# Silu in the mixer written as x·(1 + tanh(x/2)), with the product on VectorE

## The chip, the cores and the metric

The kernel runs on one core of a Trainium2 chip. Five engines work beside each other, each through its own queue in order: TensorE (PE, with its weight loads PEld), VectorE (DVE), ScalarE (ACT), GpSimd (POOL) and SyncE (SP, which only issues DMAs). An instruction that waits holds up everything behind it on its engine. The metric is the device time of one execution in microseconds; lower is better.

## The reference

One decoder layer on 512 tokens of width 1024, in float32: a SwiGLU feed-forward block, a mixer of three branches (sparse attention, gated DeltaNet, cross-attention into a memory), and a second feed-forward block. What matters here are three places of the mixer with a silu, silu(x) = x·sigmoid(x):

```python
qkv = silu(causal_depthwise_conv(dn_qkv, dn_conv_w))          # 4 taps, 3 x 4 heads x 128 channels
dq, dk, dv = split(qkv);  dq = l2_norm(dq);  dk = l2_norm(dk) # x * rsqrt(sum(x*x) + 1e-6), per head
beta = sigmoid(dn_b)
o_dn = gated_delta_rule(dq, dk, dv, log_decay, beta)          # v enters as v*beta, k as k*beta*exp(g)
o_dn = rms_norm(o_dn, dn_out_norm) * silu(dn_z)               # the output gate
# compression of keys and values in the sparse attention:
silu(blocks @ w1) @ w2
```

The feed-forward blocks have a silu too; it is not touched.

## The kernel before

**Products.** Weights are streamed from HBM in tiles of 128 x 512: SP loads the tile (`wraw`, L105), ACT rounds it to a short float (`whi`, L106), DVE, or POOL for some tiles, forms the rest (`wlo`, L109). Each product in full precision is then a triple of matmuls, high by high (L117), high by low (L118, L119). One projection of 512 columns is 8 tiles of the contraction, 24 matmuls of 512 columns into one PSUM bank (`pfm`), or, where tokens are in the partitions, into four banks (`ptm`).

**DeltaNet.** For each of 4 heads there are three convolutions (s = 0, 1, 2 for q, k, v). `dn_conv` projects into a PSUM bank, DVE multiplies it by the last tap (`cacc`, through L229) and adds the other three (L844), all reading that bank, and ACT applies Silu into `cy`. `dn_head` transposes `cy` on PE into `ptr` (L862). For v, DVE multiplies by beta into `vb`. For q and k, ACT squares with a sum (`sq`, L874), DVE takes 1/sqrt by nine tiny steps (L138 to L148) and scales (`qs` or `kn`, L880), PE transposes back (`ptk`, L887), ACT copies (L888). `dn_rows` loads a head's cumulative log decays to all partitions by a DMA from DRAM (`rowsb`, L896, on SP's queue); ACT takes `eg` = exp of it (L899), POOL subtracts and masks (L900, L901), ACT takes `dec` = exp (L902). `dn_lt` multiplies k by beta on POOL (`kbT`), PE forms k·kᵀ (`pkk`, L931), DVE multiplies by `dec` and a DMA stores it; `dn_subst` loads it for two heads (`Lb`), inverts 16 x 16 blocks by substitution on DVE (30 small instructions, `Bt` and `Bi`, L951, L953, each waiting for the one before), stores the result (`dD`, L955, issued in ACT's queue) and loads it spread out (`Dc`); `dn_double` and `dn_level` start from `Dm`, made of `Dc` on DVE (L971). `in_z` projects the output gate into four banks and ACT applies Silu (`zg`, L787). `compress` does the same on 128 x 256 (`hs`, L1159) and transposes on.

**Buffers.** `cy` has 3 buffers, `cacc` 2, `rowsb`, `eg`, `dec` and `kn` 1 each. The projections' banks come in turn from a few tags of PSUM.

**Order.** The steps are given as a list of names in the table at L37: `i` the first products, `a` the scalars (beta, decays), `c01` the convolution of head 0, s = 1, `h01` its `dn_head`, `r0` the rows, `l0` and `k0` what follows, `b0` the substitution of heads 0 and 1, `z` the output gate, `e`, `d`, `s` the doubling, levels and states, `x`, `p`, `f` the compression. Each has an offset of priority and a number that says every how many weight tiles POOL makes `wlo`. From these, and from its own estimate of each instruction's duration, the framework's scheduler deals the instructions into the engines' queues at build time. So another duration or another instruction shifts the order of all that stands around it. The table itself is the same before and after.

## Time and profile before

| | |
|---|---|
| median of 3 runs | 1307.05 us (1304.54 to 1307.46) |
| the profiled execution | 1297.11 us, span 1295.3 us |
| DeltaNet's convolutions, heads, substitution | about 400 to 545 us of the span |
| levels, states, compression | about 545 to 690 us |

The profile is of one execution, which was itself shorter than the runs' median. A row of a group reads: line of the kernel, engine, operation, output <- inputs, shape, count | busy time in us, mean ns | idle time of the engine just before these instructions, and what ended it. A row of a timeline reads: start, duration, engine, line, operation; in brackets the idle time before it and what was waited for. [...]

[...]

### The profile page before, as it was taken

What the parts mean: (1) busy time and instruction counts of PE and PEld (TensorE: products, weight loads), DVE (VectorE), ACT (ScalarE), POOL (GpSimd) and SP (SyncE); (2) the same over time, 40 slices, a digit from 0 to 9 for tenths busy, and PEclk for the clock granted to TensorE, in tenths of its full rate; (3) what the DMA queues carried; (4) which work ended last, traced back from release to release, by engine and by line L of the source; (5) the groups of instructions that cost most, each with busy time, mean ns of one, the idle gap of its engine ahead of it and who ended that gap; (6) DMA issues with size and microseconds to landing.
All of it is one profiled execution on the core that took longest, in us unless ns stands there. A gap on an engine that the chain in (4) does not pass through costs nothing. (4 is left out here: it accounts for less than half of the span.)

```text
span 1295.3 us, 21771 instructions
## 1 busy us (share of the span) xinstructions
PE 1267.4 (98%) x7959; PEld 1102.6 (85%) x7959; DVE 978.2 (76%) x1778; ACT 734.8 (57%) x1487; POOL 213.1 (16%) x225
## 2 busy tenths in 40 slices
PE   8999999999999999999999999999999999999997
PEld 7889999988787778888777788899788899999886
DVE  6898878699877865845789776665688788785988
ACT  6566666576765644416564545544576566655663
POOL 0021112130002222002111112232200121110300
PEclk8999999999999999999999999999999999999999
DMA  7757656695663341333221142232843786664963
GB/s 238 250 173 186 179 179 125 195 220 202 228 198 106 111 125 50 85 114 117 65 58 58 58 138 66 82 115 94 276 167 117 257 189 187 183 128 152 235 223 113
DMA packets 112123, 195.61 MB, mean 151 GB/s; under 512 B 18973, under 2 KB 28561, under 8 KB 112017
## 3 DMA queue, kind: packets, MB, share of 16 engines
q1 hardware_dynamic: 95856, 159.36, 37.3%
q0 software_dynamic: 15872, 34.61, 13.8%
q8 instruction: 62, 1.02, 0.3%
q10 hardware_dynamic: 288, 0.26, 0.1%
q14 instruction: 45, 0.36, 0.1%
HBM read 184.15 MB, written 33.08 MB: 168 GB/s over the span
## 5 line engine op out<-in xcount | busy, mean ns | idle before, releaser
L106 ACT CAST whi<-wraw 128x512 fp32r<-128x512 f32 (+1 forms) x226 | 136.4, 615 | 133.6 <-PE pfm L119 61.3
L109 DVE TENSOR_TENSOR wlo<-wraw,whi 128x512 fp32r<-128x512 f32 (+1 forms) x195 | 133.8, 697 | 48.1 <-ACT whi L106 46.9
L536 POOL DMA_DIRECT2D T<-in_ffn_d_dram x88 | 59.5, 677 | 375.2 <-PE pg L119 111.7
L117 PE MATMUL pfm<-xth,whi 128*128 128x512 f32 x272 | 108.1, 402 | 2.0 <-ACT whi L106 0.9
L118 PE MATMUL pfm<-xth,wlo 128*128 128x512 f32 x272 | 108.5, 404 | 1.3 <-POOL wlo L109 1.3
L119 PE MATMUL pfm<-xtl,whi 128*128 128x512 f32 x272 | 107.9, 402 | 0.0
L109 POOL TENSOR_TENSOR wlo<-wraw,whi 128x512 fp32r<-128x512 f32 x28 | 38.2, 1366 | 229.5 <-ACT whi L106 165.4
L446 PE MATMUL smm<-thi,fset 128*128 128x256 f32 x384 | 67.9, 276 | 0.0
L117 PEld LDWEIGHTS pfm<-xth,whi 128*128 128x128 f32 x272 | 51.1, 189 | 13.0 <-issue 1.8
L466 DVE TENSOR_TENSOR up<-s,smm 128x256 f32<-128x256 f32 x32 | 13.5, 422 | 61.7 <-ACT se L461 61.7
L118 PEld LDWEIGHTS pfm<-xth,wlo 128*128 128x128 f32 x272 | 50.9, 188 | 10.6 <-POOL wlo L109 1.8
L119 PEld LDWEIGHTS pfm<-xtl,whi 128*128 128x128 f32 x272 | 50.9, 188 | 9.6 <-issue 0.8
L446 PEld LDWEIGHTS smm<-thi,fset 128*128 128x128 f32 x384 | 58.0, 188 | 0.2
L655 ACT CAST ringh<-ringr 128x1024 fp32r<-128x1024 f32 (+1 forms) x44 | 45.1, 1032 | 22.0 <-PE acc_mm L673 6.7
L446 PE MATMUL smm<-thi,fxtl 128*128 128x256 f32 x192 | 53.2, 277 | 0.7 <-DVE fxtl L421 0.7
L446 PE MATMUL smm<-thi,fxth 128*128 128x256 f32 x192 | 53.0, 276 | 0.0
L446 PE MATMUL se<-thi,fset 128*128 128x256 f32 x256 | 45.2, 276 | 0.0
L1256 ACT ACTIVATE Pm<-Pm,nm 128x384 f32<-128x384 f32 (+2 forms) x64 | 35.6, 558 | 14.6 <-DVE nm L1255 14.1
L688 DVE TENSOR_TENSOR sl<-H,sh 128x1024 fp32r<-128x1024 f32 (+2 forms) x38 | 40.9, 1082 | 3.1 <-ACT sh L687 2.9
L673 PE MATMUL acc_mm<-ringh,sh 128*128 128x512 f32 x108 | 42.3, 391 | 0.0
L673 PE MATMUL acc_mm<-ringh,sl 128*128 128x512 f32 x108 | 42.1, 390 | 0.0
L687 ACT CAST sh<-H 128x1024 fp32r<-128x1024 f32 (+2 forms) x38 | 35.3, 935 | 11.6 <-PE acc_r L673 3.6
(626 smaller groups left out, 4336.4 us busy)
## 6 DMA issues: line engine op xcount, KB each, us to landing
T<-in_ffn_d_dram POOLq DMA_DIRECT2D x88, 256.0 KB, 4.2
fq<-in_ffn_g_dram SPq DMA_DIRECT2D x64, 256.0 KB, 3.4
fq<-in_ffn_u_dram SPq DMA_DIRECT2D x64, 256.0 KB, 3.8
wraw<-in_ffn_g_dram SPq DMA_DIRECT2D x34, 256.0 KB, 3.2
wraw<-in_ffn_u_dram SPq DMA_DIRECT2D x34, 256.0 KB, 3.5
wraw<-in_ffn_d_dram SPq DMA_DIRECT2D x34, 256.0 KB, 3.7
ringr<-T SPq DMA_DIRECT2D x16, 512.0 KB, 6.6
ringr<-in_ffn_d_dram POOLq DMA_DIRECT2D x16, 512.0 KB, 8.9
```

Of the source, the lines that this page charges most:

```text
L106: nc.scalar.copy(hi, raw)
L109: self.lmark = eng.tensor_tensor(lo, raw, hi.bitcast(F32), op=OP.subtract)
L117: t.matmul(out, lh, rh, start=first, stop=False)
L118: t.matmul(out, ll, rh, start=False, stop=False)
L119: self.tick(t.matmul(out, lh, rl, start=False, stop=last), 3 * math.prod(out.shape[1:]))
L446: m = lambda x, y, **kw: te.matmul(out, x, y, skip_group_check=True, **kw)
L536: i = g.dma_start(o[c], x[c], max_dma_last_dim=2048, **({"accum_op": OP.add} if add else {}))
L655: nc.scalar.copy(hi, raw)
L673: e = lambda a, b, s, f: nc.tensor.matmul(acc[i], a, b, start=s, stop=f, skip_group_check=True)
L687: nc.scalar.copy(hi, f)
L688: last = tt(low, f, hi.bitcast(F32), op=OP.subtract)
L1256: nc.scalar.activation(pm, pm, AF.Exp, bias=nm[:, qb : qb + 1], scale=-1.0, accum_out=sm[:, qb : qb + 1])
```

## The change

Since silu(x) = x·(1 + tanh(x/2))/2, each of the three places becomes a Tanh on ACT with scale 0.5 and one DVE instruction (t + 1)·x (lines 789, 850 and 1164 of the changed kernel), which yields twice the silu. The factor 2 is taken out later: `hb`, half of beta, for v; 4·EPS for EPS in the norm of q and k, which is otherwise indifferent to a factor; the gain of the output norm halved once after its load (`dnog`); 0.5 in the copy of `hT`. The factor of k in the delta rule, `nbg`, keeps beta.

```diff
     def in_z(self, uh, ul, zg):
...
-            nc.scalar.activation(zg[:, b].rearrange("p h d -> p (h d)"), p, AF.Silu)
+            z = zg[:, b].rearrange("p h d -> p (h d)")
+            nc.scalar.activation(z, p, AF.Tanh, scale=0.5)
+            nc.vector.scalar_tensor_tensor(z, z, 1.0, p, op0=OP.add, op1=OP.mult)
     def dn_scalars(self, sm, mp):
...
-        nbg = t("nbg")
+        nbg, hb = t("nbg"), t("hb")
+        v.tensor_scalar(hb, beta, 0.5, None, op0=OP.mult)
...
-        return sg, gb[:, :16].rearrange("p (n h) -> p n h", h=4), beta, nbg, dr
+        return sg, gb[:, :16].rearrange("p (n h) -> p n h", h=4), hb, nbg, dr
     def dn_conv(self, h, s, uh, ul):
...
-        nc.scalar.activation(y, ac, AF.Silu)
+        nc.scalar.activation(y, ac, AF.Tanh, scale=0.5)
+        v.scalar_tensor_tensor(y, y, 1.0, ac, op0=OP.add, op1=OP.mult)
     def dn_head(self, h, s, y, sc, dp, d):
...
-                v.tensor_tensor(d["vb"], p, beta[:, :, h, None].to_broadcast(T4), op=OP.mult)
+                v.tensor_tensor(d["vb"], p, hb[:, :, h, None].to_broadcast(T4), op=OP.mult)
...
-        r = self.rsqrt(ss, TB, 1.0, EPS, "dr")
+        r = self.rsqrt(ss, TB, 1.0, 4 * EPS, "dr")
     def compress(self, ph, cm, op_):
...
-        nc.scalar.activation(hs, ph, AF.Silu)
+        nc.scalar.activation(hs, ph, AF.Tanh, scale=0.5)
+        nc.vector.scalar_tensor_tensor(hs, hs, 1.0, ph, op0=OP.add, op1=OP.mult)
...
-        nc.vector.tensor_copy(hT, pt.rearrange("p (k w c) -> p k w c", k=2, w=2))
+        nc.vector.tensor_scalar(hT, pt.rearrange("p (k w c) -> p k w c", k=2, w=2), 0.5, None, op0=OP.mult)
                def small():
                     nc.sync.dma_start(self.cw, a["conv_w"])
                     nc.sync.dma_start(self.dnog, a["dn_og"])
+                    nc.vector.tensor_scalar(self.dnog, self.dnog, 0.5, None, op0=OP.mult)
```

The lines below the first edit move by 2 to 6. The compiled program has 17 table loads before and 3 after.

The instructions move, in the DeltaNet part above all. Three places are shown. The first is ACT's queue from the first convolution's activation to the third's (cy is the activation of a convolution, sq the squares of a norm, eg and dec the decays, whi a rounded weight tile, k the copy of the transposed k). Before:

```order
374 L846 ACT_TABLE_LOAD
375 L846 ACTIVATE cy<-cacc 128x512
376 L106 CAST whi<-wraw 128x512
377 L874 ACTIVATE sq,dss<-ptr_4474 128x128 x4
378 L106 CAST whi<-wraw 128x512
379 L899 ACT_TABLE_LOAD
380 L899 ACTIVATE eg<-rowsb 128x512
381 L902 ACTIVATE dec<-dec 128x512
382 L846 ACT_TABLE_LOAD
383 L846 ACTIVATE cy<-cacc 128x512
384 L888 COPY k<-ptk 128x512
385 L106 CAST whi<-wraw 128x512 x2
```

And with the change:

```order
374 L849 ACTIVATE cy<-cacc 128x512
375 L106 CAST whi<-wraw 128x512
376 L878 ACTIVATE sq,dss<-ptr_4478 128x128 x4
377 L106 CAST whi<-wraw 128x512
378 L903 ACTIVATE eg<-rowsb 128x512
379 L849 ACTIVATE cy<-cacc 128x512
380 L906 ACTIVATE dec<-dec 128x512
381 L106 CAST whi<-wraw 128x512
382 L892 COPY k<-ptk 128x512
383 L106 CAST whi<-wraw 128x512
```

The second convolution's activation stands between eg and dec instead of behind dec, and a weight tile follows dec at once.

The second is DVE's queue at the same place, the end of the first k norm (small steps drm, dry, drz; kn is the scaled k). Before:

```order
463 L145 SCALAR_TENSOR_TENSOR dry<-drz,dry 128x4
464 L146 TENSOR_TENSOR drz<-dry 128x4
465 L147 SCALAR_TENSOR_TENSOR drz<-drz,drm 128x4
466 L148 SCALAR_TENSOR_TENSOR dry<-drz,dry 128x4
467 L880 TENSOR_TENSOR kn<-ptr_4474,dry 128x512
468 L229 TENSOR_SCALAR cacc<-pfm,cw 128x512
```

And with the change:

```order
466 L145 SCALAR_TENSOR_TENSOR dry<-drz,dry 128x4
467 L850 SCALAR_TENSOR_TENSOR cy<-cy,cacc 128x512
468 L146 TENSOR_TENSOR drz<-dry 128x4
469 L147 SCALAR_TENSOR_TENSOR drz<-drz,drm 128x4
470 L148 SCALAR_TENSOR_TENSOR dry<-drz,dry 128x4
471 L229 TENSOR_SCALAR cacc<-pfm,cw 128x512
472 L884 TENSOR_TENSOR kn<-ptr_4478,dry 128x512
```

The second convolution's product now stands inside the norm, and the scale of the third convolution ahead of kn. On PE the four transposes of kn come five matmuls later than before.

The third is DVE's queue at the end of the first substitution, with the change; before, the pairs of Bt and Bi ran to the end with one wlo between them, and Dm (there L971) followed with no convolution open.

```order
592 L957 TENSOR_TENSOR Bi<-Bi,Bt 64x3x13
593 L789 SCALAR_TENSOR_TENSOR zg<-zg,ptm 128x512
594 L955 TENSOR_TENSOR Bt<-Lb,Bi 64x28
595 L789 SCALAR_TENSOR_TENSOR zg<-zg,ptm 128x512
596 L957 TENSOR_TENSOR Bi<-Bi,Bt 64x2x14
597 L789 SCALAR_TENSOR_TENSOR zg<-zg,ptm 128x512
...
604 L847 SCALAR_TENSOR_TENSOR cacc<-pfm,cw,cacc 128x509
605 L975 TENSOR_TENSOR Dm<-Dc,msk 128x512 x2
606 L975 TENSOR_TENSOR DT<-Dc,msk 128x512
607 L847 SCALAR_TENSOR_TENSOR cacc<-pfm,cw,cacc 128x510
608 L789 SCALAR_TENSOR_TENSOR zg<-zg,ptm 128x512
609 L847 SCALAR_TENSOR_TENSOR cacc<-pfm,cw,cacc 128x511
```

Three products of the output gate lie in the substitution, and Dm stands between the taps of the ninth convolution. ACT issues the DMA dD behind three tanh of the gate, where before it stood ahead of the gate's activations. The DMA of the third head's rowsb comes two weight tiles later on SP's queue. From about 620 us of the span on, the order is as before.

## The prediction

> **What bounds the kernel now.** I read the summary of engines first, then the busy time by stages, then TensorE's waits in the stage that is touched.

> ```profile
> span 1295.3 us, 21771 instructions
> PE 1267.4 (98%) x7959; PEld 1102.6 (85%) x7959; DVE 978.2 (76%) x1778; ACT 734.8 (57%) x1487; POOL 213.1 (16%) x225
> ```

> PE works in 98% of the span, so an edit on ACT and DVE can only gain where PE stands still for one of them. The changed instructions run almost all between 400 and 620 us. In the windows below the columns are stretch, length, then busy PE, PEld, DVE, ACT, POOL with counts, PE's clock, DMA share and GB/s.

> ```profile
> 400.00:475.60 75.60, 69.91 (x343) 56.57 (x343) 57.52 (x143) 42.49 (x92) 20.84 (x20) 1.00 0.37 110
> 475.60:545.00 69.40, 68.64 (x426) 58.07 (x425) 49.30 (x142) 28.64 (x72) 10.39 (x13) 1.00 0.24 70
> 545.00:620.00 75.00, 74.49 (x481) 61.02 (x480) 41.65 (x109) 30.80 (x79) 14.82 (x16) 1.00 0.38 117
> ```

> PE's idle time is 75.60 - 69.91 = 5.69, then 0.76, then 0.51: 6.96 us in all. That is the ceiling of any gain, whatever the edit takes off ACT. ACT is idle for 44% of the first window and more than half of the others. PE's waits in 400 to 620 us, grouped (total, times, longest):

> ```profile
> PE ptk L887 <- DVE Bi L953: 1.7, 1, 1.7
> PE pfm L118 <- POOL wlo L109: 1.3, 1, 1.3
> PE ptk L887 <- DVE qs L880: 1.0, 2, 0.9
> PE pfm L117 <- ACT whi L106: 0.9, 1, 0.9
> PE pkk L931 <- POOL kbT L909: 0.7, 1, 0.7
> ```

> Of these 5.6 us only the 0.9 names ACT. 2.7 name DVE, which gets more to do, and 2.0 name POOL.

> **ACT's side.** The operations removed and replaced:

> ```profile
> L846 ACT ACT_TABLE_LOAD x6 | 7.7, 1283 | 0.1
> L899 ACT ACT_TABLE_LOAD x4 | 5.1, 1283 | 1.4 <-DMA rowsb<-drows 1.3
> L902 ACT ACT_TABLE_LOAD x2 | 2.6, 1283 | 0.0
> L846 ACT ACTIVATE cy<-cacc 128x512 f32<-128x512 f32 x12 | 7.6, 632 | 3.1 <-DVE cacc L844 2.9
> L1332 ACT ACTIVATE tg<-up 128x512 f32<-128x512 f32 x7 | 4.4, 625 | 0.0
> L787 ACT ACTIVATE zg<-ptm 128x512 f32<-128x512 f32 x4 | 2.1, 604 | 0.0
> ```

> Silu and Exp alternate in this stage, and each change of function puts a load of 1.283 us ahead. The order below has 14 fewer loads: these 12, one before zg and one at L1200. 14 x 1.283 = 18.0 us of ACT go. The Tanh that stands in for Silu costs the same: the kernel has it already (tg, 625 ns against 632 for cy).

> [...]

> **DVE's side.** Each Tanh gets a product (t + 1)·x on DVE. The same operation is in the trace at L1337, from SBUF and PSUM; L844 is the next.

> ```profile
> L1337 DVE SCALAR_TENSOR_TENSOR tg<-tg,pfm 128x512 f32<-128x512 f32 x16 | 10.3, 682 | 6.3 <-ACT tg L1332 3.6 <-POOL wlo L109 2.7
> L844 DVE SCALAR_TENSOR_TENSOR cacc<-pfm,cw,cacc 128x511 f32<-128x511 f32 x12 | 9.0, 746 | 0.2
> L951 DVE TENSOR_TENSOR Bt<-Lb,Bi 64x15 f32<-64x15 f32 x4 | 0.7, 166 | 0.4 <-DMA Lb<-dL 0.3
> ```

> The z products are L1337's form: 4 x 0.68 = 2.7. The convolutions' product reads two SBUF operands; I take 0.69, with 0.75 as upper bound: 12 x 0.69 = 8.3, at most 9.0. The compression's, half as wide, is at most 0.4 and the two small ones (beta and the norm's gain halved) are about 0.2 each, by the 166 ns of a tiny operation. Together 11.8 us. The other edits ride in instructions that exist: 4·EPS for EPS is a constant, and halved beta is another operand, so they cost nothing. The copy of hT is one DVE pass as before.

> [...]

> ```profile
> 462.98 1.05 DVE L951 TENSOR_TENSOR Bt<-Lb,Bi 64x55 f32<-64x55 f32 x1
> 462.50 1.47 POOL L916 TENSOR_TENSOR kd<-kn,dec 128x512 f32<-128x512 f32 x1 [3.44 <-DVE Bi L953]
> 468.64 0.21 DVE L951 TENSOR_TENSOR Bt<-Lb,Bi 64x55 f32<-64x55 f32 x1
> ```

> The same instruction takes 1.05 while POOL works, 0.21 otherwise: 0.84 for a collision. POOL is busy 46.05 of these 220 us (20.84 + 10.39 + 14.82), 21%, so of 12 products some 2.5 meet it: 2 us more on DVE, not on PE's path unless DVE is late there. [...]

> **Where PE feels it.** The instruction order around these stages is dealt anew, so I walked the queues.

> *First head's k, 407 to 420 us.* In this listing come start, duration, engine, instruction.

> ```profile
> 408.17 1.28 ACT L899 ACT_TABLE_LOAD   x1
> 410.82 0.63 ACT L899 ACTIVATE eg<-rowsb 128x512 f32<-128x512 f32 x1 [1.37 <-DMA rowsb<-drows]
> 413.39 0.63 ACT L902 ACTIVATE dec<-dec 128x512 f32<-128x512 f32 x1 [1.94 <-POOL dec L901]
> 414.04 1.28 ACT L846 ACT_TABLE_LOAD   x1
> 415.34 0.63 ACT L846 ACTIVATE cy<-cacc 128x512 f32<-128x512 f32 x1
> 416.34 1.14 ACT L106 CAST whi<-wraw 128x512 fp32r<-128x512 f32 x2
> 409.57 0.17 DVE L146 TENSOR_TENSOR drz<-dry 128x4 f32<-128x4 f32 x1
> 410.17 0.69 DVE L880 TENSOR_TENSOR kn<-ptr,dry 128x512 f32<-128x512 f32 x1
> 410.50 0.39 PE L119 MATMUL pfm<-xtl,whi 128*128 128x512 f32 x1
> 410.92 0.66 PE L887 MATMUL ptk<-cst,kn 128*128 128x128 f32 x4
> 415.54 0.39 PE L117 MATMUL pfm<-xth,whi 128*128 128x512 f32 x1
> 415.76 0.39 PE L118 MATMUL pfm<-xth,wlo 128*128 128x512 f32 x1
> 417.01 0.50 PE L117 MATMUL pfm<-xth,whi 128*128 128x512 f32 x1 [0.86 <-ACT whi L106]
> 419.08 0.50 PE L118 MATMUL pfm<-xth,wlo 128*128 128x512 f32 x1 [1.33 <-POOL wlo L109]
> ```

> Here the load does hurt: after dec ends at 414.02, load and cy and a copy keep the next whi until 416.34, and PE waits 0.86 and, behind it for the rest of that weight, 1.33. In the new order whi follows dec at once, at 414.0, 2.3 us earlier, and both waits go: 2.2 us, with the restarts about 2.5.

> But the new order hangs something else there. DVE's queue holds the product of the second convolution between the fourth and the fifth small step of the k norm (behind L145). Its tanh stands on ACT behind eg, and eg still waits for the DMA rowsb until 410.82. So: tanh 411.4 to 412.0, product to 412.7, the norm's three last steps 0.6 (410.17 - 409.57), a scale of the next convolution 0.7 that is now also ahead, kn at 414.0, and the transposes 0.75 later (410.92 - 410.17): 414.75. PE has five matmul rows more in front, which start 0.22 apart (415.54, 415.76), so it comes at 410.73 + 5 x 0.22 = 411.8. A new wait of 2.9 us. Term: 2.9 - 2.5 = +0.4. If tanh and product slip in earlier than I think, it falls to -2.5; if POOL collides with the product, it is +1.2.

> *The q and k norms behind.* The transposes of qs (1.0 in two waits) come once one product later, 0.68 at most, of which I take 0.4 (PE has as many rows in front as before); at the other place the order has 18 rows of the next convolution ahead of them, and that wait of 0.9 goes. kbT (0.7): +0.2, one product in the k chain less the loads. The 1.7 behind Bi: DVE has the product there too and PE five rows fewer, but the small steps of the norm are no longer interleaved with the substitution: -0.3. Sum: -0.6, bounds -2.5 and +1.5.

> *The output gate, from 460 us.*

> ```profile
> 471.76 0.67 ACTq L955 DMA_DIRECT2D dD<-Bi  x1
> 475.00 2.07 ACT L787 ACTIVATE zg<-ptm 128x512 f32<-128x512 f32 x4
> 477.98 2.16 DVE L971 TENSOR_TENSOR Dm<-Dc,msk 128x512 f32<-128x512 f32 x2 [3.49 <-DMA Dc<-dD]
> 406.50 2.73 SPq L105 DMA_DIRECT2D wraw<-in_w_dn_dram  x2
> ```

> Two things make the substitution later. The third head's row DMA stands two weight loads further back on SP, 2.73 us by the last row, and the substitution waits for the decays made from it; with the squares behind eg I take 4 us. Then three of the four zg products lie inside the substitution's last steps, 3 x 0.68 = 2.0. The DMA dD, which ACT now issues behind three tanh, goes from 471.76 to 477.8, and Dm from 477.98 to about 484. PE itself does not use Dm at once. But the ninth convolution's DVE work now lies around Dm: the bank that it reads comes free at 484 + 2.8 (Dm, DT) + 2 x 0.75 + 0.68 = 489. PE wants that bank two convolutions later: 475.7 + 2 x 24 x 0.22 = 486.3, with transposes between about 488. Term: +1.0. The ninth convolution itself needs a z bank that is freed by the first zg product, and that sits behind most of the substitution: +0.5, bounds 0 and +2.3.

> *The rest.* L1200's load lies where PE waits for DVE, not for it: 0. The compression's tanh and product: ACT's 0.38 becomes 0.8, beside PE's projections: 0. Without that cover it would cost 0.4.

> **Sum.** +0.4 - 0.6 + 1.0 + 0.5 = +1.3 us. The profiled execution took 1297.11, with 1.8 around its span of 1295.3; it would take 1298.4. The median of the runs is 1307.05, 9.9 above that execution, and I carry that over: 1308.4.

> **The rivals.** *Faster:* the loads were what made everything late, and the new waits do not arise, since tanh and product follow closer than I walked. Then the 0.9 and 1.3, with restarts 2.5, most of the 1.0 and half of the 1.7 go: about -4, 1303; -7 at the very most. For it: the chain at 414 to 419 shows a load on PE's path. Against it: 1.7 + 1.0 of the waits name DVE.

> *Slower, by the substitution:* dD is issued not at 477.8 but later, since DVE (busy 57.52 of 75.60 in that window, plus some 8 us of products, so 87%) meets POOL and stands behind the tanh of z, in its own queue. From about 479 on, each microsecond comes through to PE, by the ninth convolution's bank and then by the products that read Dm. With 3 to 4 us more of delay: +1.3 + 3.5 = about +5, 1312. For it: DVE would be the densest engine after PE there, and stalls in order. Against it: behind 475.6 PE idles 0.76 of 69.40 in the old order, so this stage has had slack. [...]

> *Nothing:* ACT was idle enough and DVE too, the schedules cancel, 1307; it falls within the forecast's bounds.

> **How the numbers follow.** What a measurement of this kernel can tell from no change is about 0.2%, 2.6 us. The forecast and the case of nothing, both within that: 0.42. Faster: 0.23. Slower, by the substitution or by the first head's wait at its upper bound: 0.35, more than the faster case, since three of four terms that I could walk point there. The likeliest case alone spans 1305.5 to 1311 by its bounds; with the rivals, 1302.5 to 1313.5.

> **What would show it.** Three table loads are left, ACT's busy time falls by about 18, DVE's rises by about 12. PE has a wait of 2 to 3 us at ptk <- kn near 412 to 415, and none for whi and POOL's wlo near 417. dD is issued near 478, and PE waits about 1 us for cacc in the third convolution after z. It would be wrong if ptk <- kn waits under 1 us (then the faster case), if PE's idle time in 475 to 545 grows beyond 3 us (the slower one), or if the products run far from 0.69.

## The result, and the profile after

The changed kernel is slower: its median is 1318.18 us (8 runs, 1310.66 to 1321.64) against 1305.16 for the kernel before (8 runs, 1298.33 to 1307.46). The ratio is 1.0111, 95% interval 1.0086 to 1.0137. The forecast of 1308.4 with a range up to 1313.5 was too low. The profiled execution took 1317.94.

The summary of engines of the changed kernel, and the three windows that the prediction showed of before (stretch, length, busy PE, PEld, DVE, ACT, POOL with counts, PE's granted clock, DMA share, GB/s):

```profile
span 1316.2 us, 21780 instructions
PE 1281.4 (97%) x7959; PEld 1112.0 (84%) x7959; DVE 993.1 (75%) x1797; ACT 717.2 (54%) x1473; POOL 213.6 (16%) x225
...
400.00:475.60 75.60, 66.29 (x319) 53.67 (x318) 59.10 (x133) 29.38 (x79) 19.47 (x18) 0.97 0.34 99
475.60:545.00 69.40, 66.49 (x384) 55.83 (x382) 52.41 (x131) 20.54 (x47) 11.74 (x15) 0.98 0.27 77
545.00:620.00 75.00, 73.15 (x482) 58.15 (x482) 41.39 (x134) 23.51 (x79) 8.13 (x9) 1.00 0.27 84
```

ACT's busy time falls by 17.6 us and DVE's rises by 14.9. ACT has 1473 instructions where it had 1487: the 14 loads are gone. The groups of the changed instructions:

```profile
L849 ACT ACTIVATE cy<-cacc 128x512 f32<-128x512 f32 x12 | 7.5, 628 | 12.2 <-DVE cacc L847 12.2
L850 DVE SCALAR_TENSOR_TENSOR cy<-cy,cacc 128x512 f32<-128x512 f32 x12 | 9.0, 754 | 3.7 <-ACT cy L849 3.6
```

The Tanh costs what the Silu did (628 against 632 ns). So the work changed as planned, and the time did not follow.

To find the loss I cut out one stage: from PE's first product with the running sums of the decays (`pgc`) to its first product of the compressed attention (`pcl`). Before, and after:

```profile
400.01 0.40 PE L820 MATMUL pgc<-ld,cst 128*128 128x16 f32 x2 [0.33 <-DVE ld L817]
606.63 1.00 PE L1194 MATMUL pcl<-cbd,qT 128*128 128x64 f32 x8
...
400.01:606.63 206.62, 200.18 (x1182) 165.28 (x1183) 137.03 (x369) 92.56 (x222) 41.72 (x45) 1.00 0.31 94
```

```profile
403.62 0.40 PE L822 MATMUL pgc<-ld,cst 128*128 128x16 f32 x2 [0.33 <-DVE ld L819]
623.34 1.00 PE L1199 MATMUL pcl<-cbd,qT 128*128 128x64 f32 x8
...
403.62:623.34 219.72, 205.98 (x1181) 168.01 (x1182) 151.88 (x386) 76.03 (x209) 42.51 (x45) 0.98 0.30 88
```

The stage takes 13.1 us longer (219.72 - 206.62), close to the difference of the medians (13.0). The two profiled executions as wholes lie further apart, 20.9 us (1316.2 - 1295.3): runs of the same kernel differ by several us, and the profiled one of before was shorter than its median. So below I compare this stage. PE's idle time in it goes from 6.44 to 13.74, +7.3; the rest, +5.8, is PE at work for longer on the same matmuls. PE's waits after:

```profile
PE ptk L891 <- DVE Bt L955: 3.5, 1, 3.5
PE ptk L891 <- DVE kn L884: 3.3, 1, 3.3
PE ptk L891 <- DVE qs L884: 1.5, 1, 1.5
PE pkk L935 <- POOL kbT L913: 1.3, 2, 0.7
PE pfm L117 <- DVE cacc L847: 1.2, 1, 1.2
PE pot L1064 <- DVE on L1058: 1.0, 1, 1.0
```

The first row is the third k norm, the second the first. At the first, the timeline reads:

```profile
414.17 0.63 ACT L903 ACTIVATE eg<-rowsb 128x512 f32<-128x512 f32 x1 [2.41 <-DMA rowsb<-drows]
414.70 0.61 ACT L849 ACTIVATE cy<-cacc 128x512 f32<-128x512 f32 x1
415.35 0.69 DVE L850 SCALAR_TENSOR_TENSOR cy<-cy,cacc 128x512 f32<-128x512 f32 x1 [2.40 <-ACT cy L849]
415.96 1.22 DVE L146 TENSOR_TENSOR drz<-dry 128x4 f32<-128x4 f32 x1
418.89 0.66 PE L891 MATMUL ptk<-cst,kn 128*128 128x128 f32 x4 [3.26 <-DVE kn L884]
...
416.29:419.70 3.41, 0.81 (x6) 0.78 (x7) 3.31 (x7) 1.26 (x3) 2.29 (x4) 1.00 0.00 0
419.70:423.11 3.41, 3.41 (x10) 2.64 (x9) 2.20 (x3) 1.61 (x3) 3.41 (x3) 0.50 0.26 79
```

The DMA's wait is handed on: eg waits 2.41 for it, the tanh stands behind eg, the product behind the tanh, the rest of the norm behind the product, and PE waits 3.26. The small step L146 (415.96 to 417.18) also took 1.22 instead of 0.17 while POOL worked (L905, 415.41 to 417.17). And then comes what I had not priced: the granted clock falls to 0.50 for the 3.41 us of the last row, in which PE is busy throughout. In it the matmuls of 512 columns start 0.43 us apart (419.95, 420.38), at clock 1.00 they start 0.23 apart with records of 0.39 that overlap (413.42, 413.65). By the granted clock such a dip loses half its length, 1.7 us, which is an estimate; by the starts it would be 1.6. The stage has two after, here and at the third k norm, and none before. Together they lose 3.4 us. So of the +5.8, 3.4 are clock. The other 2.4 I come back to.

At the third k norm, ACT's and DVE's rows and the clock behind them:

```profile
469.42 0.63 ACT L903 ACTIVATE eg<-rowsb 128x512 f32<-128x512 f32 x1 [1.87 <-DMA rowsb<-drows]
470.34 0.23 DVE L138 TENSOR_SCALAR drm<-dss 128x4 f32<-128x4 f32 x1 [4.17 <-ACT sq L878]
...
470.90:474.31 3.41, 0.17 (x1) 0.00 (x0) 3.13 (x9) 1.14 (x2) 1.14 (x2) 1.00 0.29 48
474.31:477.73 3.42, 3.17 (x12) 2.92 (x13) 3.32 (x9) 0.59 (x1) 1.58 (x2) 0.50 0.23 83
```

Here the squares stand on ACT behind an eg that waits for its DMA, and DVE stands idle for 4.17 us until the squares are done.

### The profile page after: what moved, and what is told of

Its sections match the earlier page's. It is cut to its first block, busy times and chain, and to the rows that moved or that the text cites. A ratio compares the mean times of both kernels' runs of the same rounds, so it can differ in the third digit from the quotient of the medians.

```text
span 1316.2 us, 21780 instructions
## 1 busy us (share of the span) xinstructions
PE 1281.4 (97%) x7959; PEld 1112.0 (84%) x7959; DVE 993.1 (75%) x1797; ACT 717.2 (54%) x1473; POOL 213.6 (16%) x225
## 3 DMA queue, kind: packets, MB, share of 16 engines
q0 software_dynamic: 15872, 34.61, 13.7%
## 5 line engine op out<-in xcount | busy, mean ns | idle before, releaser
L106 ACT CAST whi<-wraw 128x512 fp32r<-128x512 f32 (+1 forms) x226 | 136.7, 616 | 138.8 <-PE pfm L119 67.3
L109 DVE TENSOR_TENSOR wlo<-wraw,whi 128x512 fp32r<-128x512 f32 (+1 forms) x195 | 134.4, 699 | 46.0 <-ACT whi L106 44.9
L117 PE MATMUL pfm<-xth,whi 128*128 128x512 f32 x272 | 109.3, 406 | 2.6 <-DVE cacc L847 1.2
L118 PE MATMUL pfm<-xth,wlo 128*128 128x512 f32 x272 | 108.7, 404 | 0.0
L119 PE MATMUL pfm<-xtl,whi 128*128 128x512 f32 x272 | 108.2, 402 | 0.0
L109 POOL TENSOR_TENSOR wlo<-wraw,whi 128x512 fp32r<-128x512 f32 x28 | 37.2, 1328 | 231.1 <-ACT whi L106 165.7
L117 PEld LDWEIGHTS pfm<-xth,whi 128*128 128x128 f32 x272 | 51.4, 190 | 13.6 <-issue 2.2
L119 PEld LDWEIGHTS pfm<-xtl,whi 128*128 128x128 f32 x272 | 51.4, 190 | 9.2
L118 PEld LDWEIGHTS pfm<-xth,wlo 128*128 128x128 f32 x272 | 51.2, 190 | 8.9
L687 ACT CAST sh<-H 128x1024 fp32r<-128x1024 f32 (+2 forms) x38 | 35.3, 936 | 11.8 <-PE acc_r L673 3.6
```

The lines of the kernel that those rows point to most:

```text
L106: nc.scalar.copy(hi, raw)
L109: self.lmark = eng.tensor_tensor(lo, raw, hi.bitcast(F32), op=OP.subtract)
L117: t.matmul(out, lh, rh, start=first, stop=False)
L118: t.matmul(out, ll, rh, start=False, stop=False)
L119: self.tick(t.matmul(out, lh, rl, start=False, stop=last), 3 * math.prod(out.shape[1:]))
L687: nc.scalar.copy(hi, f)
```

## The experiments

All in one table. "Idle" is PE's idle time, and "clock" what the dips lose (an estimate: half their length, at the granted clock of 0.50), in the stage of each kernel's profile. "Order" says in whose order the queues stand.

| kernel | order | ratio to before (95%) | stage us | idle | clock |
|---|---|---|---|---|---|
| before | old | 1 | 206.6 | 6.4 | 0.0 |
| the change | new | 1.0111 (1.0086-1.0137) | 219.7 | 13.7 | 3.4 |
| new_ops_old_order | old | 1.0071 (1.0043-1.0098) | 214.6 | 12.7 | 1.7 |
| old_ops_new_order | new | 1.0057 (1.0029-1.0084) | 215.8 | 9.7 | 3.4 |
| product_behind_kn | new, edited | 1.0089 (1.0057-1.0122) | 221.0 | 13.9 | 5.1 |
| kn_and_squares_first | new, edited | 1.0044 (1.0015-1.0072) | 214.4 | 10.3 | 1.7 |
| no_products_old_order | old | 1.0028 (1.0005-1.0051) | 208.2 | 7.9 | 0.0 |
| products_off_path_old_order | old | 1.0037 (1.0012-1.0061) | 214.3 | 10.1 | 5.1 |
| old_kernel_plus_products | old | 1.0044 (1.0013-1.0076) | 211.8 | 9.4 | 3.4 |
| new_convs_only_old_order | old | 1.0078 (1.0040-1.0116) | 213.4 | 11.5 | 1.7 |
| new_ops_first_tap_on_scalar | old | 1.0082 (1.0055-1.0109) | 214.9 | 12.8 | 1.7 |
| change_first_tap_on_scalar | own | 1.0121 (1.0077-1.0165) | 222.2 | 13.1 | 5.1 |
| change_two_rowsb | own | 1.0081 (1.0052-1.0109) | 218.0 | 13.7 | 1.7 |
| new_ops_retimed | old, edited | 1.0064 (1.0045-1.0083) | 212.6 | 10.5 | 1.7 |
| new_ops_retimed_2 | old, edited | 1.0018 (0.9989-1.0048) | 211.1 | 9.1 | 1.7 |
| new_ops_retimed_3 | old, edited | 1.0037 (1.0020-1.0054) | 211.6 | 9.1 | 1.7 |
| new_convs_retimed | old, edited | 1.0072 (1.0048-1.0096) | 210.9 | 10.5 | 0.0 |
| change_idle_matmuls | new | 1.0102 (1.0081-1.0123) | 218.0 | 9.4 | 1.7 |
| before_exp_behind_squares | old, edited | 1.0001 (0.9976-1.0025) | 208.8 | 7.0 | 1.7 |

A stage time is of one execution, a ratio of 4 to 12 runs. The two can lie some 5 us apart: new_convs_retimed is at +4.3 by its stage and at about +9 by its ratio. So the traces show where time goes, and differences of a few us between two kernels are no verdict.

An order is held by order-only links between neighbours of each engine's list, which add no semaphore (before_exp_behind_squares, which has them, is at 1.0001):

```diff
+    for names in ORDER.values():
+        for a, b in zip(names, names[1:]):
+            tc.add_manual_dep(find(b), find(a), NoSync)
```

**The operations or the order?** The change brings both. new_ops_old_order holds the changed kernel's five queues in the order of before, with the new DVE instructions free to fall in; old_ops_new_order holds the kernel before in the order of the change.

> The changed kernel, with all instructions of all five engines held in the order of the kernel before; only the 19 added VectorE instructions are placed freely, each behind its tanh. If the changed order is what costs (theory), the two waits of 3.3 and 3.5 us for kn and the low clock behind them are gone, and with 14 table loads fewer the kernel is at or below the one before: -4 to +1 us. If the added work on VectorE costs (rival), whatever the order, it stays slower than before by 6 to 13 us.

> The kernel before, Silu and its 17 table loads kept, no product on VectorE, with all instructions held in the order of the changed kernel. If the order costs by itself, it is slower than before by 5 to 14 us. If the added work costs, or only order and product together (the product inside the norm, behind a tanh that stands behind eg), it is within 3 us of before.

Each alone loses: +8.0 and +9.2 us in the stage, against +13.1 for both. Neither alone explains the loss, and they don't add up. In new_ops_old_order, ACT's and DVE's rows at the first k norm, and the waits:

```profile
412.11 0.63 ACT L906 ACTIVATE dec<-dec 128x512 f32<-128x512 f32 x1 [1.93 <-POOL dec L905]
413.30 1.12 DVE L850 SCALAR_TENSOR_TENSOR cy<-cy,cacc 128x512 f32<-128x512 f32 x1 [2.92 <-ACT cy L849]
...
PE ptk L891 <- DVE qs L884: 3.3, 2, 2.4
PE ptr L866 <- DVE cy L850: 2.5, 2, 2.0
PE pfm L117 <- DVE cacc L847: 1.9, 1, 1.9
```

No load stands here any more, but DVE waits 2.92 for a tanh whose queue waits for POOL. In the kernel before, Silu behind dec held up only ACT. Now DVE's queue is tied to it, and what stands behind the product (qs, the next cacc) reaches PE late. In old_ops_new_order, which has neither a tanh nor a product, the third k norm waits as long as in the change:

```profile
PE ptk L887 <- DVE Bt L951: 3.8, 1, 3.8
```

So the wait at the third k norm belongs to the order. The one at the first needs both: in neither of these two kernels does the first kn keep PE waiting. Its place with the new operations alone is taken by the 1.9 for `cacc`.

**Taking away the two long waits, in the new order.** The product of the second convolution goes behind the first kn; then, in the second kernel, the third eg also goes behind the squares.

```diff
-DVE: ... L145  L850 #2  L146 L147 L148 L229 L884 #1 ...
+DVE: ... L145  L146 L147 L148 L229 L884 #1  L850 #2 ...
```
```diff
-ACT: ... L903 #3  L878 (four squares) ...
+ACT: ... L878 (four squares)  L903 #3 ...
```

> The changed kernel in its own order, one instruction moved: the product of the second convolution stands behind the first kn, not inside its norm. If the first place costs what the trace says (3.3 us of waiting, and 1.7 us of matmuls at a lower clock behind it), the wait for the first kn falls under 1 us, and the kernel gains 3 to 5 us on the changed one. If the time only moves to the next wait (whi and wlo, as before), it gains under 1.5 us.

> As the one with the product behind kn, and one more instruction moved: on ScalarE the exp of the third head's rowsb stands behind the last square of the k norm, not ahead of it. If that exp, waiting for its DMA, made the third kn late, the wait of 3.5 us there falls to about 1.2, the clock stays up, and it gains another 3 to 4 us: 6 to 9 less than the changed kernel. If the norm is late for VectorE's own work, the wait stays above 2.5.

The first removed its wait, and the stage did not get shorter (221.0; the ratio, 1.0089, can't be told from the change's): a wait of 2.2 for `on` and longer dips near 563 took back what was won. With both, the stage is 5.3 shorter than the change's, and by the ratios, too, this is a gain (1.0044 against 1.0111, and the intervals do not meet). But the third kn still waits 3.32, which I had not expected. In that kernel:

```profile
451.40 1.27 POOL L913 TENSOR_TENSOR kbT<-k,rowsb 128x512 f32<-128x512 f32 x1 [0.29 <-ACT k L892]
452.70 0.38 SPq L900 DMA_DIRECT2D rowsb<-drows  x1
458.68 0.63 ACT L903 ACTIVATE eg<-rowsb 128x512 f32<-128x512 f32 x1 [1.70 <-DMA rowsb<-drows]
459.86 0.69 DVE L109 TENSOR_TENSOR wlo<-wraw,whi 128x512 fp32r<-128x512 f32 x1 [2.07 <-ACT whi L106]
```

The row buffer is the link: the third head's rows are asked for only when kbT of the second has read the one buffer (451.40 + 1.27, then 452.70), and they land some 5.9 us later. eg waits for them, whi stands behind eg, and a wlo behind whi stands in DVE's queue inside the norm.

**A second row buffer** (`bufs=1` to `bufs=2` for `rowsb`, the order dealt anew by the framework), in the change and in the kernel before:

> The changed kernel with two buffers for rowsb in place of one; the scheduler deals the order itself. The third head's row DMA was issued only when kbT of the second had read the one buffer. If that made the third kn late (theory), that wait of 3.5 us falls under 1.5 us, with the low clock behind it: 3 to 5 us less than the changed kernel. If the chain is late elsewhere, it gains under 1 us.

> The kernel before with two buffers for rowsb, the scheduler's own order. The wait of 1.7 us for the third kn was partly for that DMA: -1 to -2 us if it goes; with a new order, as for the change, anything from -3 to +5.

The third kn's wait fell from 3.5 to 1.2, yet the stage fell only by 1.7 and PE's idle time not at all: other waits took its place, among them 2.4 for zg. For the kernel before the ratio is 1.0057 (1.0027 to 1.0087): it got slower. In its trace the clock stands at half for 37 us on end, so the stage is not compared.

**Is it DVE's extra time or where the products stand?** One kernel leaves the convolutions' products out (so `cy` is the bare tanh), one puts them into a tile that nothing reads (so `cy` is the bare tanh there too), one adds such unread products to the kernel before.

```diff
-        v.scalar_tensor_tensor(y, y, 1.0, ac, op0=OP.add, op1=OP.mult)
+        cx = self.da.tile([P, SEQ], F32, tag="cx", name="cx", bufs=1)
+        v.scalar_tensor_tensor(cx, ac, 1.0, ac, op0=OP.add, op1=OP.mult)
```

> Leaves out the 12 products of the convolutions (cy is tanh alone); the other edits stand; all instructions in the order of the kernel before. It shows what 14 table loads fewer are worth alone. If removing the loads helps at all, the waits 0.9 and 1.3 near 417 us go, and it is 2 to 5 us faster than before (theory: the gain is there, and the products eat it). If the loads were hidden (rival), it is within 1.5 us of before.

> As the one without products, but 12 instructions of the product's form and size run on VectorE all the same, (x+1)*x from cacc into a scratch tile that nothing reads; cy is tanh alone, so the result is not the reference's. The new operations in the old order lost about 8 us between 400 and 620 us against before. If VectorE's added time does that (rival), this kernel is as slow, 6 to 9 us over before. If the hop VectorE to ScalarE to VectorE on the way to the transposes does it, and VectorE standing in its queue for the tanh (theory), it is within 2 us of the kernel without products.

> The kernel before, whole (Silu, 17 table loads, its order), plus 12 instructions (x+1)*x from cacc into a scratch tile, which nothing reads: VectorE's added time alone, 12 x 0.69 us, with no tanh, no hop and no new order. If VectorE is the second bound among the convolutions (its busy share is 95% at 432 to 452 us), it loses 4 to 8 us between 400 and 620 us. If VectorE had room, as its 73% over 400 to 560 says, it loses under 1.5 us.

Without the convolutions' products the stage is 1.5 us longer than before, with all 14 loads gone from ACT (the products of the gate and the compression are still there). This is the plainest run on the loads: taking them away gained nothing in this order. Of the 0.9 + 1.3 for whi and wlo near 417 us, 0.4 is left, and these waits are new or longer:

```profile
PE ptk L890 <- DVE Bi L956: 2.3, 1, 2.3
PE ptr L865 <- ACT cy L849: 1.2, 1, 1.2
PE pfm L118 <- DVE wlo L109: 1.1, 1, 1.1
```

Products that nobody waits for still bring +7.7 (products_off_path_old_order), of which 5.1 are three dips; by the ratios, 1.0037 against 1.0028, the kernel can't be told from the one that leaves them out. Added to the kernel before, they cost +5.2 us, of which 3.4 are clock and 1.8 the rest, and here the ratio says so too: 1.0044, with an interval above 1. There they lie on no path to PE but DVE's queue, and PE waits 2.3 at two norms:

```profile
PE ptk L889 <- DVE kn L882: 2.3, 1, 2.3
PE ptk L889 <- DVE Bi L955: 2.3, 1, 2.3
```

DVE's cover there is thin: between 432 and 452 us of the kernel before, DVE is busy for 19.01 of 20.00.

```profile
432.00:452.00 20.00, 18.37 (x100) 15.02 (x99) 19.01 (x42) 13.05 (x30) 6.00 (x5) 1.00 0.26 81
```

**Giving DVE its time back.** The first tap of each convolution (L229, 12 x 0.75 = 9.0 us) goes to ACT, which has room since the loads left. If DVE's time were the cause, this would return the loss. Once in the old order, once in an order dealt anew; and one kernel with the convolutions alone changed, z and the compression with Silu:

```diff
-        self.scale(PRM.get("cva", "v"), ac, p, self.cw[:, j, 3:4])
+        self.scale(PRM.get("cva", "s"), ac, p, self.cw[:, j, 3:4])
```

> The new operations in the old order, and the first multiplication of each convolution (cacc from the bank, 0.745 us) goes from VectorE to ScalarE, which the loads left with time: VectorE gives back 12 x 0.75 us for the 12 x 0.69 of the products. If VectorE's time is what costs, the loss of 7.7 us between 400 and 620 us falls to 0 to 2.5. If the longer chain from bank to transposes costs, or ScalarE becomes late, it stays above 5.

> The changed kernel with the first multiplication on ScalarE, dealt by the scheduler itself. VectorE has as much as before, ScalarE about 10 us less than before: -3 to +3 us against before if the new order is harmless now, +4 to +9 if the scheduler's order costs as it did with the old operations (8 us).

> The new form in the 12 convolutions alone; output gate and compression keep Silu; order of the kernel before. The new operations in the old order lost 7.7 us between 400 and 620 us. If the convolutions' products do it, 4 to 7 us are left here; if the gate's products on VectorE, among the substitution, do it, under 3.

It returned nothing: +8.3 against +8.0 in the old order, and +15.6 against +13.1 in an order of its own, above both cases that I had named. DVE now waits longer for ACT, here between 400 and 500 us of new_ops_first_tap_on_scalar (5.1 and 4.0 in new_ops_old_order):

```profile
DVE wlo L109 <- ACT whi L106: 8.9, 8, 3.1
DVE cy L850 <- ACT cy L849: 4.7, 4, 3.3
```

So moving a piece of DVE's work to ACT does not help. It does not clear DVE's time of the loss: the tap went to the engine that DVE waits for, and the unread products cost 1.0044 by themselves. The convolutions alone make +6.7 of the +8.0, so the gate and the compression are at most a small part.

**Placing the same work better.** In the old order, the second convolution's tanh goes ahead of the eg that it waited behind, the sixth's ahead of a dec, and the products behind what PE waits for (behind qs, kn), with z's last two behind the ninth convolution's product:

```diff
-ACT: ... L903 #1 ... L906 #1  L849 #2 ...
+ACT: ... L849 #2  L903 #1 ... L906 #1 ...
-DVE: ... L850 #7 ... L884 (kn) ...
+DVE: ... L884 (kn)  L850 #7 ...
```

> The new operations in the old order on TensorE, GpSimd and SyncE, with the same work on VectorE and ScalarE; only two tanh go ahead of an exp that waits for GpSimd or a DMA, and eight products go behind what TensorE waits for next (kn, qs, the taps of the ninth convolution, X). If the place in the queue costs (theory), the loss of 7.7 us between 400 and 620 us falls to -2 to +2, no clock under 1 there. If VectorE's added time itself costs (rival; 5.2 alone), it stays at 4 or more.

> The same moves with the new form in the convolutions alone (gate and compression keep Silu). By the place theory -2 to +1.5 us between 400 and 620, against 6.5 without the moves; by the time theory 4 or more. If the gate's products matter, it is 1 to 2 us better than the retimed kernel with all three places.

> As the retimed kernel, but the product of the twelfth convolution stands between the X again, as in the old order with the new operations. By the place theory the wait of 3.2 us near 532 and the low clock behind it go, the wait for X is back at about 1.2, and the loss between 400 and 620 us falls from 5.7 to about 2.5 us. By the time theory it stays at 4 or more.

> As the second retimed one; GpSimd makes the first wlo before kd and kbT, and the third head's exp of rowsb, which waits 2.2 us for its DMA, stands behind the squares and the weight tile on ScalarE. The waits of 1.3 (wlo) and 2.3 us (third kn) go or fall under 0.7: -1.5 to +1 us against before between 400 and 620. Over the whole kernel no difference from before that can be told; if placement is not the cause, 3 or more lost.

The first of them put one product wrong: the twelfth, behind the compression's X, where PE's `ptr` then waited 3.1 for the queue. With it back in its old place (new_ops_retimed_2) the stage is at +4.5, of which 1.7 are clock, and the ratio is 1.0018, which can't be told from 1. Its longest wait, 2.0, is again at the third k norm. Moving the third eg, and POOL's weight tile, as well (new_ops_retimed_3) gave nothing more: the third kn waited 2.7, kbT 1.25.

The same instructions thus cost 8.0 us of the stage in one order and 4.5 in another. But all four of these kernels lose more than 4 us there, where I had named 4 or more (3 for the last) as the sign that placement is not the cause. So placement returns a part at most; the 4.5 that stay are near the 5.2 of unread products, and I take them for DVE's added time, which is not shown apart. No order that I tried beat the kernel before.

**The third eg in the kernel before.** Behind the squares and the next weight tile, no other edit:

> The kernel before, with the one move on ScalarE: the third head's exp of rowsb behind the squares and the weight tile. Its wait of 1.7 us for the third kn falls under 0.7; 1 us gained between 400 and 620, too little for the whole kernel to tell. If the wait is for VectorE's substitution, as its row names it, nothing changes.

I had expected a shorter wait at the third kn; it rose from 1.7 to 2.4. In the substitution DVE now waits 1.0 for the DMA `Lb`, which is made from what eg and dec lead to; that this is the reason is not tested:

```profile
PE ptk L887 <- DVE Bi L953: 2.4, 1, 2.4
DVE Bt L951 <- DMA Lb<-dL: 1.0, 1, 1.0
...
420.83:424.24 3.41, 1.43 (x6) 0.57 (x4) 1.33 (x2) 2.75 (x6) 2.67 (x3) 1.00 0.02 5
424.24:427.65 3.41, 3.41 (x11) 2.86 (x12) 2.55 (x4) 0.00 (x0) 1.52 (x1) 0.50 0.47 136
```

The last two rows are another matter: at the first head, where the edit reaches nothing, PE has the same two waits as before, for whi and wlo, and here the clock falls behind them. In the kernel before it did not:

```profile
417.16:420.57 3.41, 2.08 (x8) 1.39 (x9) 2.68 (x4) 1.36 (x3) 3.41 (x3) 1.00 0.29 78
```

**The clock by itself.** I looked for what decides a dip. In every run's records the clock changes only at multiples of 3.413 us from one another, as if windows of that length ran through the whole execution (in the change the two dips begin at 419.70 and 474.31, 54.61 apart, 16 times 3.413). So I cut PE's rows at these marks, in all traces but that of before_two_rowsb with its 37 us. Of 23 dips in the touched stage, 21 follow a window in which PE was idle for 1.90 us or more; no window with so much idle time was without one, and the most without is 1.89. (The other two dips, both near 560 us, follow windows with 1.3 and 1.5. Two of the 23 last for two windows, with 1.0 and 0.3 of idle time in their first, so this count does not explain everything.) So a wait is dear by where it falls. The longest that cost nothing more is 3.15 us, in new_convs_retimed, with a mark in its middle, so that it gives 1.82 to the one window and 1.33 to the next:

```profile
538.41:541.82 3.41, 1.59 (x7) 0.95 (x6) 3.19 (x12) 0.04 (x1) 0.00 (x0) 1.00 0.02 7
541.82:545.23 3.41, 2.08 (x11) 1.82 (x12) 2.12 (x8) 1.35 (x7) 0.00 (x0) 1.00 0.00 0
```

At the same two waits, before_exp_behind_squares and before differ in just this: 1.98 of idle time in the one window (3.41 - 1.43), 1.33 in the other.

As a test, in the change's own order, ten matmuls into a bank that nothing reads go ahead of the transposes of the first and the third kn, so that PE has work while it waits:

```diff
+        if (h, s) in {(0, 1), (2, 1)}:
+            idle, u = self.bank("s", "idle"), self.uh
+            for i in range(10):
+                te.matmul(idle, u[:, 0, :P], u[:, 0], start=i == 0, stop=i == 9)
```

> The changed kernel in its own order, with 10 matmuls of 512 columns (2.3 us) that nobody reads on TensorE just ahead of the transposes of the first and of the third kn, where it waits 3.3 and 3.5 us. kn comes when it comes, so the waits end at the same time. If the low clock behind these waits is due to the idle time (theory), the granted clock stays at 1.0 there and it is 2.5 to 3.5 us faster than the changed kernel. If the clock falls all the same, it gains nothing; if the transposes come later by the idle work, it loses.

Both dips are gone. The stretch that held the first, and two waits:

```profile
414.00:426.00 12.00, 12.00 (x62) 9.98 (x61) 10.15 (x24) 4.92 (x14) 5.05 (x4) 1.00 0.47 139
...
PE ptk L897 <- DVE Bt L961: 1.6, 1, 1.6
PE pfm L119 <- DVE zg L791: 1.2, 1, 1.2
```

At the first place 2.7 us are won; at the third a wait of 1.2 for zg takes the win back, and one dip arises at 563. The total (1.0102) can't be told from that of the change (1.0111). So the clock is a real part of a long wait's price, but only a part of the loss.

## Why the prediction was wrong

**Right.** *ACT's side:* 14 loads and 18 us went, and nothing came of it for the end. *DVE's side:* 11.8 us forecast and some 2 more for collisions with POOL, 14.9 measured. The median product of a convolution takes 684 ns, as I took it; the mean of 754 comes from one of 1.51 beside POOL's `wlo`. *First head's k:* the new wait, forecast 2.9 behind rowsb, eg, tanh and product, is 3.26 by that very chain (with 1.05 in it from the L146 that met POOL, which I had not placed there), and the two waits for whi and wlo went. *The output gate:* forecast 1.0 at the third convolution behind z, measured 1.2 (`cacc`) by the walked chain of Dm and the taps; that the size came out is in part luck, since the bank (498.4 for 489) and PE (497.3 for 488) both come some 9.4 us later than I walked. Forecast 0.5 for the bank of the ninth, measured 0.1.

**The step that failed** is "The q and k norms behind", forecast -0.6. "That wait of 0.9 goes": it became 1.5. The rows that the new order puts ahead of it on PE cover nothing: old_ops_new_order, which has them and no product, waits 0.86 there, as before. The products add the other 0.6. I had not seen that DVE has 19.01 of 20.00 us taken there, so that a product pushes the whole queue; my 87% was an average over 75.6 us. "The 1.7 behind Bi ... -0.3": it became 3.5. I had seen that the small steps of the norm were no longer interleaved with the substitution and took it for a gain. But in the new order the norm begins only when ACT has passed an eg that waits for the row DMA, and the next weight tile is in that line too. I had used that DMA's delay ("I take 4 us") for the substitution only, not for the norm behind it. And the delay was larger. The issues of the third head's row DMA before and after:

```profile
451.00 0.38 SPq L896 DMA_DIRECT2D rowsb<-drows  x1
463.66 0.38 SPq L900 DMA_DIRECT2D rowsb<-drows  x1
```

Counted from the stage's first product that is 51.0 and 60.0 us, 9 later. It is not SP's weight loads that hold it, as I had walked: in both kernels it is issued 0.03 us behind the end of the second head's kbT, which reads the one row buffer (450.97 and 463.63). In old_ops_new_order it comes at 55.2, and the third kn waits 3.8 there, so the order alone is enough for this wait. Together with kbT (1.3 for 0.7) this term is about +2.9 in waits (0.5 + 1.8 + 0.6), instead of -0.6.

**The term that was missing** is the clock. My sum had a wait of 2.9 cost 2.9. Two of the waits, 3.26 and 3.5, lay for the most part in one window each and brought a dip: +3.4.

**"The rest: 0"** failed too, in smaller pieces: 1.0 for `on`, 0.8 in two waits for Bi, 0.4 for `vn`, some 2.2 together, in stages that the new order and the later substitution reach.

By the balance: idle time grew by 7.3 where the sum had +1.3; 3.4 are clock. The last 2.4 lie within PE's busy time. Busy time less clock is 202.6 in the change, 202.7 with the old operations in the same order and 202.6 with two row buffers, but 200.2 before and 200.2 with the new operations in the old order: it goes with the order. If each matmul is given only the time by which its record runs past the end of those ahead of it, the small ones (up to 128 columns) take 3.6 us more than before in the change, as much in old_ops_new_order and 0.2 in new_ops_old_order; those of 512 columns take 1.2 less in the change. So in the new order the records of small matmuls cover each other less.

**The rivals.** The slower rival had the side right and the place wrong. dD is issued at 487.1, far later than the 477.8 that I walked, but from 475.6 to 545 PE idles 2.91 us, just below the 3 that I had set as its sign: PE had been held up about as long ahead of it. The faster rival is not borne out by no_products_old_order: with the loads gone and no product in the convolutions, the stage is still 1.5 us longer, and the ratio is 1.0028. One rival was not tried: the table of steps and priorities stayed as it was for the old operations, and one made for the new ones may deal a better order.

## What to carry to other kernels

An operation split over two engines ties their queues together: before giving VectorE a factor that ScalarE computed, list what stands ahead of it on ScalarE (here an exponential behind a DMA) and what stands behind the product on VectorE, and check VectorE's load in the 20 us around, not its mean. Where a scheduler deals the order, price the new order by itself: here the old operations in it lost 9 us of the stage (ratio 1.0057). And a new wait on TensorE of some 2 to 4 us may cost an estimated 1.7 more than its length by the clock, depending on where it falls in the windows (here one of 3.26 did, one of 3.15 in new_convs_retimed did not).

## What the runs showed of the hardware

Taking 14 table loads of 1.283 us each off ACT gained nothing in a kernel in which PE is busy for 98% (no_products_old_order, 1.0028).

Three DVE instructions ran longer while POOL worked: L146 of the change 1.22 instead of 0.17 us (415.96, POOL's L905 from 415.41 to 417.17), a product of the change 1.51 instead of 0.68 (422.23, POOL's `wlo` from 421.90 to 423.19), and a product of new_ops_old_order 1.12 instead of 0.69 (413.30, POOL's `kbT` from 413.02 to 414.32).
